# A retention and HGRN2 decoder layer: the last product of the down projection in two pieces of tokens, 256 and then 128

## The chip, the cores and the metric

The kernel runs on one core of a Trainium2 chip. The metric is the time of one execution on the device in microseconds; the kernel before has a median of 2376.54 us over three runs (2375.79 to 2379.05). Engines are named as in the profile: PE is TensorE's matmuls, PEld its weight loads, DVE VectorE, ACT ScalarE, POOL GpSimd, SP SyncE, which issues the DMAs here.

## What is computed

One layer of a decoder over 2048 tokens of a prompt and 8 samples of 8 tokens, width 1024. The part that matters here is the end of the layer: the squared-ReLU MLP with its residual, and the final norm.

```python
xp = xp + mp
hp = rmsnorm(xp, norm_ffn_w[l])
xp = xp + jnp.square(jax.nn.relu(hp @ w_up[l])) @ w_down[l]
...
y_prompt = rmsnorm(xp, final_norm_w)
```

The norm divides each token by the root of the mean of its 1024 squares and multiplies by one weight per column, so no token can leave before all 1024 of its columns are there.

## The kernel before, in words

Activations lie transposed: a column of the model on a partition, tokens along the free dimension. The 2112 tokens are cut into three groups (576, 768 and 768), which pass the MLP one after the other. A group is cut into two halves of T2 tokens (384 in the last group), and each large product is computed by a Strassen-like scheme of seven products on quarters of the operands. Operands are split into a rounded part `hi` and the rest `lo`, both fp32r, and a product is three matmuls: hi with hi, hi with lo, lo with hi.

`down` (L2185) is the down projection. For each of four steps `o` it runs seven such products, `LAST_OCTET` in the last step. The results are kept in slabs `g.R[v][q]`, each with two blocks of 128 columns of the model side by side; `last_block(g, n, h)` (L2360) is block `n` of half `h`. The very last of the 28 products is ("A12", "B21"). In the last group it is taken out of the loop and computed by `last_product` (L2242), and it concerns the four blocks 0 to 3 of half 0 alone, for 384 tokens each. Everything else has its final value by then: half 1 is finished by `finish` (L2276, multiplications at L2302, stores at L2304), and blocks 4 to 7 of half 0 have their squares summed in `g.sq` and their final weight multiplied in by `last_rows` (L2338).

`last_product` takes four PSUM banks, one per block (tiles called `pj` and `pf`), makes 12 matmuls of 384 columns into each (helper line L1849), and adds the result to the residual on DVE (L2259). Beside this, `finish_last` (L2364) works off the norm of half 0. It sets steps by `later(d, fn)`, at d ticks from its call; a tick is two matmuls. The steps are:

- `squares` (L2375): the squares of blocks 0 and 1 on ACT (L2377), plus `g.sq` on DVE (L2378).
- `weigh` (L2372): the final weight of a block on ACT (L2373).
- `split`: the two halves of that sum are added on DVE (L2018), rounded on ACT (L670), and the rest taken on DVE (L671).
- `square` of blocks 2 and 3, one by one, on ACT (L2385).
- `add` and `sums`: sums over the partitions by matmuls with ones on TensorE; the two squares in f32 (L2394), the two rounded parts in fp32r (L2389), all four into one bank `pj`.
- `outs` (L2396): the factor by a logarithm and an exponential on ACT (L2335, L2336), then for each pair of blocks one multiplication of 128 x 768 on DVE (L2401) and one store of 384 KB by SP (L2402).

The kernel is recorded by a scheduler: steps are put to the engines in the order in which it places them, each engine works off its own queue strictly in order, and a wait holds all that stands behind it on that engine.

Of the kernel before, what the change touches and what calls it, by code (L numbers as in the profile page):

```python
# [12 lines left out]
AF = mybir.ActivationFunctionType  # L13
ALU = mybir.AluOpType

P = 128
# [37 lines left out]
NO = NQ // 2  # L54

N_VAL = 4
N_MADE = 4
LEADS = (slice(0, 256), slice(256, WT))
N_KEPT = W_OUT0 + 4
# [146 lines left out]
class Kernel:  # L206
# [958 lines left out]
    def values_direct(self, g, p, b):  # L1165
# [7 lines left out]
        assert n <= len(banks)  # L1173
        for m in range(N_VAL):
            w = self.next_weight()
# [1065 lines left out]

    def last_product(self, g, B):  # L2242

        nc, T2 = self.nc, g.T // 2
        w = [self.next_weight(), self.next_weight()]

        banks = [self.mm(T2) for _ in range(4)]
        self.finish_last(g)
        for v in range(2):
            for i in range(2):  # L2250
                ps = banks[2 * v + i]
                for e in range(2):
                    for f in range(2):
                        c = (2 * e + f) * 256 + i * P
                        for q, (a, b) in enumerate(((0, 0), (0, 1), (1, 0))):
                            self.matmul(ps, w[v][a][:, c:c + P], self.pair(g, g.d[NO - 1][e][B][b])[:, f],
                                        start=e == f == q == 0, stop=e == f == 1 and q == 2)
                r = self.last_block(g, 2 * v + i, 0)
                nc.vector.tensor_tensor(out=r, in0=ps, in1=r, op=ALU.add)  # L2259

    def ffn(self, g, nxt, wait=0):
        g.u = {}
# [98 lines left out]
        np_, i = divmod(n, 2)  # L2361
        return self.pair(g, g.R[np_ % 2][np_ // 2, h])[:, i]

    def finish_last(self, g):  # L2364


        nc, w = self.nc, g.T // 2
        x = {}
        b2 = lambda t: t[:, :2 * w].rearrange("p (i t) -> p i t", i=2)
        block = lambda n: self.last_block(g, n, 0)  # L2370

        def weigh(n):  # L2372
            nc.scalar.activation(block(n), block(n), AF.Copy, scale=self.vec[:, V_FIN + n:V_FIN + n + 1])  # L2373

        def squares():  # L2375
            t = x["sum"] = self.get()
            nc.scalar.activation(b2(t), self.pair(g, g.R[0][0, 0]), AF.Square)  # L2377
            nc.vector.tensor_tensor(out=b2(t), in0=b2(t), in1=self.pair(g, g.sq), op=ALU.add)  # L2378

        def split():  # L2380
            x["parts"] = self.pair_parts(g, x["sum"])

        def square(n):
            x[n] = self.get()
            nc.scalar.activation(x[n][:, :w], block(n), AF.Square)  # L2385

        def sums():
            for part in x["parts"]:
                nc.tensor.matmul(x["ps"], self.ones_r, part, start=False, stop=False)  # L2389

        def add(n):
            if n == 2:
                x["ps"] = self.mm(w)
            nc.tensor.matmul(x["ps"], self.ones, x[n][:, :w], start=n == 2, stop=n == 3)  # L2394

        def outs():  # L2396
            t = self.get()
            self.last_factor(x["ps"], t[:, :w])
            for np_ in range(4):
                r = self.pair(g, g.R[np_ % 2][np_ // 2, 0])  # L2400
                nc.vector.tensor_tensor(out=r, in0=r, in1=t[:, :w].unsqueeze(1).to_broadcast([P, 2, w]), op=ALU.mult)  # L2401
                nc.sync.dma_start(self.outputs(g, 0)[:, 2 * np_:2 * np_ + 2], r)  # L2402

        for d, fn, *a in ((13, squares), (14, weigh, 0), (15, weigh, 1), (17, split), (19, square, 2), (23, add, 2),
                          (25, square, 3), (26, weigh, 2), (27, weigh, 3), (28, sums), (29, add, 3), (30, outs)):
            self.later(d, fn, *a)


# [61 lines left out]
```

## Time and profile before

| what | value |
|---|---|
| median of three runs (lowest, highest) | 2376.54 us (2375.79, 2379.05) |
| span of the profiled execution, first to last instruction | 2374.9 us |
| mean granted TensorE clock over the span | 0.998 |
| PE, PEld, DVE, ACT busy | 99%, 97%, 76%, 52% |
| from the last product's first matmul to the end of the span | 22.3 us |
| from its last result to the end of the span | 13.8 us |

The time of the profiled execution itself is not given apart from its span; the runs are other executions. Busy shares are means over the whole program. The change lies in the last one per cent of it, so the rows of that stretch are what is to be read: the windows and the timeline from 2352 us on, and the chain that ends last.

### The profile page before, as it was taken

The numbers are of one execution on the slowest core, as the hardware profiler recorded it, in microseconds if no ns is written. First come the engines' busy times: TensorE is split into PE (matmuls) and PEld (weight loads), VectorE is DVE, ScalarE is ACT, GpSimd is POOL, SyncE is SP. The second block draws the span as 40 slices with busy tenths as digits, with TensorE's granted clock in tenths as the row PEclk, the third lists the DMA queues.
The fourth block names the chain that finished last, engine by engine and source line by source line (L and its number), as shares of the span: only waits on it lengthen the run. The fifth ranks groups of instructions, "written<-read, shape, count | busy, mean of one in ns | idle before, by whom it ended". The sixth has DMA issues, their size and how long they took to land.

```text
span 2374.9 us, 39309 instructions
## 1 busy us (share of the span) xinstructions
PE 2348.4 (99%) x15322; PEld 2308.2 (97%) x15322; DVE 1795.9 (76%) x2299; ACT 1230.7 (52%) x1974; POOL 149.6 (6%) x202
## 2 busy tenths in 40 slices
PE   9999999999999999999999999999999999999998
PEld 8888799999999999999999999999999999999997
DVE  8666776777766766668769998666998786669887
ACT  5555565556655565536455556444544364445443
POOL 4222201101101010000000000000000000000000
PEclk9999999999999999999999999999999999999999
DMA  8888797778965787898777765766655458675641
GB/s 289 288 293 287 251 317 256 261 286 302 321 236 204 283 293 254 332 315 320 230 245 263 232 217 175 256 210 222 234 188 195 146 193 265 199 235 177 206 154 67
DMA packets 232505, 575.60 MB, mean 242 GB/s; under 512 B 24179, under 2 KB 92659, under 8 KB 232310
## 3 DMA queue, kind: packets, MB, share of 16 engines
q1 hardware_dynamic: 232166, 572.98, 70.7%
q8 instruction: 122, 2.00, 0.3%
q14 instruction: 73, 0.60, 0.1%
q10 hardware_dynamic: 144, 0.02, 0.0%
HBM read 419.95 MB, written 151.66 MB: 241 GB/s over the span
## 4 chain that ended last, share of the span: by engine, by line
PE 90%; DVE 3%; DMA 3%; ACT 2%; issue 1%; POOL 1%; SPq 0%; DVEq 0%; ACTq 0%
PE pj L1849 36%; PE pf L1849 28%; PE pj L452 9%; PE pj L1108 9%; PE pj L1192 2%; PE mm L1689 1%; PE mm L1697 1%; PE mm L1691 1%; PE mm L1466 1%; PE mm L1192 1%; PE mm L1619 1%; PE mm L1377 1%; PE mm L1838 1%; DMA raw<-w 0%; DMA ld<-fo 0%
## 5 line engine op out<-in xcount | busy, mean ns | idle before, releaser
L1849 PE MATMUL pj<-slab,hi 128*128 128x384 f32 (+1 forms) x3504 | 853.7, 326 | 1.1 <-ACT slab L1031 0.8
L310 ACT CAST hi<-raw 128x1024 fp32r<-128x1024 f32 (+1 forms) x449 | 471.0, 1049 | 681.4 <-PE pj L1849 266.7
L318 DVE TENSOR_TENSOR lo<-raw,hi 128x1024 fp32r<-128x1024 f32 (+1 forms) x449 | 549.6, 1224 | 164.1 <-ACT hi L310 152.6
L1849 PE MATMUL pf<-slab,hi 128*128 128x384 f32 (+1 forms) x2768 | 652.4, 321 | 0.0
L1849 PEld LDWEIGHTS pj<-slab,hi 128*128 128x128 f32 x3504 | 614.6, 188 | 1.7 <-ACT slab L1031 1.2
L1849 PE MATMUL pj<-slab,lo 128*128 128x384 f32 (+1 forms) x1752 | 570.5, 326 | 0.0
L1849 PEld LDWEIGHTS pf<-slab,hi 128*128 128x128 f32 x2768 | 480.6, 188 | 0.1
L1849 PE MATMUL pf<-slab,lo 128*128 128x384 f32 (+1 forms) x1384 | 443.1, 320 | 0.0
L1849 PEld LDWEIGHTS pj<-slab,lo 128*128 128x128 f32 x1752 | 329.3, 188 | 0.0
L1108 PE MATMUL pj<-hi,slab 128*128 128x256 f32 x1344 | 261.5, 287 | 2.0 <-DVE slab L1123 1.1
L1849 PEld LDWEIGHTS pf<-slab,lo 128*128 128x128 f32 x1384 | 260.1, 188 | 0.0
L452 PE MATMUL pj<-slab,hi 128*128 128x288 f32 (+1 forms) x1280 | 257.1, 316 | 1.7 <-ACT slab L716 0.9
L1108 PEld LDWEIGHTS pj<-hi,slab 128*128 128x128 f32 x1344 | 215.2, 191 | 3.1 <-ACT slab L1439 1.0
L452 PEld LDWEIGHTS pj<-slab,hi 128*128 128x128 f32 x1280 | 204.8, 189 | 5.4 <-issue 1.9
L1108 PE MATMUL pj<-lo,slab 128*128 128x256 f32 x672 | 190.1, 283 | 0.1
L1941 ACT CAST slab<-slab 128x768 fp32r<-128x768 f32 (+1 forms) x192 | 145.6, 780 | 63.9 <-DVE slab L1952 47.4
L1945 DVE TENSOR_TENSOR slab<-slab 128x768 fp32r<-128x768 f32 (+1 forms) x192 | 167.5, 887 | 13.2 <-ACT slab L1941 4.7
L452 PE MATMUL pj<-slab,lo 128*128 128x288 f32 (+1 forms) x640 | 149.4, 314 | 0.3 <-DVE lo L318 0.3
L1108 PEld LDWEIGHTS pj<-lo,slab 128*128 128x128 f32 x672 | 128.7, 191 | 0.3 <-DMA lo<-fki1VA12lo 0.3
L452 PEld LDWEIGHTS pj<-slab,lo 128*128 128x128 f32 x640 | 107.6, 188 | 0.7 <-DVE lo L318 0.6
L2195 DVE TENSOR_TENSOR slab<-pf,slab 128x768 f32<-128x768 f32 (+1 forms) x87 | 76.6, 885 | 24.4 <-PE pf L1849 24.3
L2195 DVE TENSOR_TENSOR slab<-pj,slab 128x768 f32<-128x768 f32 (+1 forms) x79 | 70.1, 889 | 20.5 <-PE pj L1849 20.3
(269 smaller groups left out, 2615.4 us busy)
## 6 DMA issues: line engine op xcount, KB each, us to landing
raw<-w SPq DMA_DIRECT2D x255, 512.0 KB, 4.7
slab<-fu SPq DMA_DIRECT2D x64, 384.0 KB, 5.2
fu<-ld SPq DMA_DIRECT2D x60, 384.0 KB, 4.1
ld<-x SPq DMA_DIRECT2D x40, 384.0 KB, 5.1
ld<-fin SPq DMA_DIRECT2D x28, 384.0 KB, 4.9
slab<-fu SPq DMA_DIRECT2D x32, 288.0 KB, 4.6
fu<-ld SPq DMA_DIRECT2D x30, 288.0 KB, 3.2
fres<-slab SPq DMA_DIRECT2D x16, 384.0 KB, 5.0
```

What stands on the lines that cost most here:

```text
L310: self.nc.scalar.copy(self.wts[j][0][:, c], raw[:, c])
L318: self.nc.vector.tensor_tensor(out=lo[:, c], in0=raw[:, c], in1=hi.bitcast(F32)[:, c], op=ALU.subtract)
L452: self.nc.tensor.matmul(pj[:, i, :T2], w, a[:, c0:c1], start=j == 0 and q == 0, stop=j == n - 1 and q == 2)
L1108: self.nc.tensor.matmul(ps[:, tb * 256:(tb + 1) * 256], t, w[:, cols], start=first and kb == j == 0 and tb != 1, stop=kb == KB // 2 - 1 an ...
L1192: nc.tensor.matmul(dst, t[:, s:s + C], ww, start=kb == 0 and q == 0, stop=last and q == 2, skip_group_check=True)
L1377: nc.tensor.transpose(ps[:, j * P:(j + 1) * P], src[:, c], self.ident)
L1466: nc.tensor.matmul(ps[:, j * P:(j + 1) * P], k[:, cols[c]], q[:, cols[c]], start=True, stop=True)
L1619: nc.tensor.matmul(ps[:, j * P:(j + 1) * P], rk[:, cols[c]], rq[:, cols[c]], start=True, stop=True)
L1849: self.nc.tensor.matmul(*a, **k)
L1941: self.nc.scalar.copy(hi[:, :g.T], B[name][:, :g.T])
L1945: self.nc.vector.tensor_tensor(out=lo[:, :g.T], in0=B[name][:, :g.T], in1=hi.bitcast(F32)[:, :g.T], op=ALU.subtract)
L2195: nc.vector.tensor_tensor(out=r, in0=ps, in1=r, op=ALU.add)
```

## The change

The 384 tokens of the last product are cut into `ENDS`, 256 and 128. For each piece in turn `last_product` calls `finish_last` for that piece and makes all 48 matmuls of the piece, so that 48 matmuls of 384 columns become 48 of 256 and 48 of 128. A block's two pieces go to the two banks of one double tile (`tile2`), and the piece's sum over the partitions goes to unused columns 256 and on of the first bank of tile `k` (tile 0 for the first piece, tile 1 for the second). The norm, the multiplications and the stores are made per piece: 8 multiplications and 8 stores, of 256 KB and 128 KB, instead of 4 and 4. `outs` becomes `factor` and four steps `out`, set two ticks apart.

```diff
@@ -54,6 +54,7 @@
 NO = NQ // 2
 
 N_VAL = 4
+ENDS = ((0, 256), (256, 384))
 N_MADE = 4
 LEADS = (slice(0, 256), slice(256, WT))
 N_KEPT = W_OUT0 + 4
@@ -2241,22 +2242,23 @@
 
     def last_product(self, g, B):
 
-        nc, T2 = self.nc, g.T // 2
+        nc = self.nc
         w = [self.next_weight(), self.next_weight()]
 
-        banks = [self.mm(T2) for _ in range(4)]
-        self.finish_last(g)
-        for v in range(2):
-            for i in range(2):
-                ps = banks[2 * v + i]
-                for e in range(2):
-                    for f in range(2):
-                        c = (2 * e + f) * 256 + i * P
-                        for q, (a, b) in enumerate(((0, 0), (0, 1), (1, 0))):
-                            self.matmul(ps, w[v][a][:, c:c + P], self.pair(g, g.d[NO - 1][e][B][b])[:, f],
-                                        start=e == f == q == 0, stop=e == f == 1 and q == 2)
-                r = self.last_block(g, 2 * v + i, 0)
-                nc.vector.tensor_tensor(out=r, in0=ps, in1=r, op=ALU.add)
+        tiles = [self.tile2() for _ in range(4)]
+        for k, (c0, c1) in enumerate(ENDS):
+            self.finish_last(g, c0, c1, tiles[k][:, 0, 256:256 + c1 - c0])
+            for v in range(2):
+                for i in range(2):
+                    ps = tiles[2 * v + i][:, k, :c1 - c0]
+                    for e in range(2):
+                        for f in range(2):
+                            c = (2 * e + f) * 256 + i * P
+                            for q, (a, b) in enumerate(((0, 0), (0, 1), (1, 0))):
+                                self.matmul(ps, w[v][a][:, c:c + P], self.pair(g, g.d[NO - 1][e][B][b])[:, f, c0:c1],
+                                            start=e == f == q == 0, stop=e == f == 1 and q == 2)
+                    r = self.last_block(g, 2 * v + i, 0)[:, c0:c1]
+                    nc.vector.tensor_tensor(out=r, in0=ps, in1=r, op=ALU.add)
 
     def ffn(self, g, nxt, wait=0):
         g.u = {}
@@ -2361,24 +2363,27 @@
         np_, i = divmod(n, 2)
         return self.pair(g, g.R[np_ % 2][np_ // 2, h])[:, i]
 
-    def finish_last(self, g):
-
-
-        nc, w = self.nc, g.T // 2
+    def finish_last(self, g, c0, c1, ps):
+
+
+        nc, w = self.nc, c1 - c0
         x = {}
         b2 = lambda t: t[:, :2 * w].rearrange("p (i t) -> p i t", i=2)
-        block = lambda n: self.last_block(g, n, 0)
+        two = lambda t: self.pair(g, t)[:, :, c0:c1]
+        block = lambda n: self.last_block(g, n, 0)[:, c0:c1]
 
         def weigh(n):
             nc.scalar.activation(block(n), block(n), AF.Copy, scale=self.vec[:, V_FIN + n:V_FIN + n + 1])
 
         def squares():
             t = x["sum"] = self.get()
-            nc.scalar.activation(b2(t), self.pair(g, g.R[0][0, 0]), AF.Square)
-            nc.vector.tensor_tensor(out=b2(t), in0=b2(t), in1=self.pair(g, g.sq), op=ALU.add)
+            nc.scalar.activation(b2(t), two(g.R[0][0, 0]), AF.Square)
+            nc.vector.tensor_tensor(out=b2(t), in0=b2(t), in1=two(g.sq), op=ALU.add)
 
         def split():
-            x["parts"] = self.pair_parts(g, x["sum"])
+            both = b2(x["sum"])
+            nc.vector.tensor_tensor(out=both[:, 0], in0=both[:, 0], in1=both[:, 1], op=ALU.add)
+            x["parts"] = self.parts(both[:, 0], w)
 
         def square(n):
             x[n] = self.get()
@@ -2386,23 +2391,23 @@
 
         def sums():
             for part in x["parts"]:
-                nc.tensor.matmul(x["ps"], self.ones_r, part, start=False, stop=False)
+                nc.tensor.matmul(ps, self.ones_r, part, start=False, stop=False)
 
         def add(n):
-            if n == 2:
-                x["ps"] = self.mm(w)
-            nc.tensor.matmul(x["ps"], self.ones, x[n][:, :w], start=n == 2, stop=n == 3)
-
-        def outs():
-            t = self.get()
-            self.last_factor(x["ps"], t[:, :w])
-            for np_ in range(4):
-                r = self.pair(g, g.R[np_ % 2][np_ // 2, 0])
-                nc.vector.tensor_tensor(out=r, in0=r, in1=t[:, :w].unsqueeze(1).to_broadcast([P, 2, w]), op=ALU.mult)
-                nc.sync.dma_start(self.outputs(g, 0)[:, 2 * np_:2 * np_ + 2], r)
-
-        for d, fn, *a in ((13, squares), (14, weigh, 0), (15, weigh, 1), (17, split), (19, square, 2), (23, add, 2),
-                          (25, square, 3), (26, weigh, 2), (27, weigh, 3), (28, sums), (29, add, 3), (30, outs)):
+            nc.tensor.matmul(ps, self.ones, x[n][:, :w], start=n == 2, stop=n == 3)
+
+        def factor():
+            x["t"] = self.get()
+            self.last_factor(ps, x["t"][:, :w])
+
+        def out(np_):
+            r = two(g.R[np_ % 2][np_ // 2, 0])
+            nc.vector.tensor_tensor(out=r, in0=r, in1=x["t"][:, :w].unsqueeze(1).to_broadcast([P, 2, w]), op=ALU.mult)
+            nc.sync.dma_start(self.outputs(g, 0)[:, 2 * np_:2 * np_ + 2, c0:c1], r)
+
+        for d, fn, *a in ((13, squares), (14, weigh, 0), (15, weigh, 1), (17, split), (19, square, 2), (23, add, 2), (25, square, 3),
+                          (26, weigh, 2), (27, weigh, 3), (28, sums), (30, add, 3), (31, factor),
+                          (34, out, 0), (36, out, 1), (38, out, 2), (40, out, 3)):
             self.later(d, fn, *a)
 
 
```

Where the steps stand in the queues is told by the built program. Slabs 21266 and 21381 hold blocks 0 and 1 and blocks 2 and 3, slabs 21320 and 21448 blocks 4 to 7; `pj_24550`, `pj_24551`, `pf_24552` and `pf_24553` are the product's four tiles, slab 24593 the first sum of squares, 24674 the second piece's, and 24640, 24654 and 24721 hold the factors. On DVE, the end of the queue from the add of block 2 on, before:

```order
L2259 TENSOR_TENSOR slab_21381<-pf_24552,slab_21381 128x384
L2018 TENSOR_TENSOR slab_24593<-slab_24593 128x384
L2259 TENSOR_TENSOR slab_21381<-pf_24553,slab_21381 128x384
L671 TENSOR_TENSOR slab_24607<-slab_24593,slab_24607 128x384
L2401 TENSOR_TENSOR slab_21266<-slab_21266,slab_24640 128x768
```

And the end of the same queue now, from the adds of the second piece's first two blocks on:

```order
L2261 TENSOR_TENSOR slab_21266<-pj_24551,slab_21266 128x128
L2405 TENSOR_TENSOR slab_21266<-slab_21266,slab_24654 128x2x256
L2405 TENSOR_TENSOR slab_21381<-slab_21381,slab_24654 128x2x256
L2381 TENSOR_TENSOR slab_24674<-slab_24674,slab_24518 128x256
L2405 TENSOR_TENSOR slab_21320<-slab_21320,slab_24654 128x2x256
L2405 TENSOR_TENSOR slab_21448<-slab_21448,slab_24654 128x2x256
L2385 TENSOR_TENSOR slab_24674<-slab_24674 128x128
L2261 TENSOR_TENSOR slab_21381<-pf_24552,slab_21381 128x128
L672 TENSOR_TENSOR slab_24692<-slab_24674,slab_24692 128x128
L2261 TENSOR_TENSOR slab_21381<-pf_24553,slab_21381 128x128
L2405 TENSOR_TENSOR slab_21266<-slab_21266,slab_24721 128x2x128
```

The second piece's halving add (L2385) and its adds of blocks 2 and 3 (L2261) stand behind the first piece's four multiplications (L2405). On PE, the end of the last product before, with the sums by ones behind it:

```order
L1849 MATMUL pf<-slab,hi 128x384 x2
L1849 MATMUL pf<-slab,lo 128x384
L2394 MATMUL pj<-slab,ones 128x384
L2389 MATMUL pj<-slab,ones_r 128x384 x2
L2394 MATMUL pj<-slab,ones 128x384
```

And now, from the eighth matmul of the second piece on; the fences show the first piece's sums, and then the end:

```order
L1850 MATMUL pj<-slab,hi 128x128 x2
L2397 MATMUL pj<-slab,ones 128x256
L1850 MATMUL pj<-slab,hi 128x128 x2
L1850 MATMUL pj<-slab,lo 128x128
```

```order
L1850 MATMUL pf<-slab,hi 128x128
L2397 MATMUL pj<-slab,ones 128x128
L1850 MATMUL pf<-slab,hi 128x128
L1850 MATMUL pf<-slab,lo 128x128
L2394 MATMUL pj<-slab,ones_r 128x128 x2
L2397 MATMUL pj<-slab,ones 128x128
```

The first piece's first sum by ones stands behind eight matmuls of the second piece, with the other 40 behind it; the second piece's first sum stands before the last two matmuls of the product.

## The prediction

> **What bounds the kernel now.** I read the page first, then the end of the program: busy time by stretch, the chain of waits, and the rows of the single operations. The page's span, busy times and chain by engine:
>
> ```profile
> span 2374.9 us, 39309 instructions
> PE 2348.4 (99%) x15322; PEld 2308.2 (97%) x15322; DVE 1795.9 (76%) x2299; ACT 1230.7 (52%) x1974; POOL 149.6 (6%) x202
> PE 90%; DVE 3%; DMA 3%; ACT 2%; issue 1%; POOL 1%; SPq 0%; DVEq 0%; ACTq 0%
> ```
>
> TensorE is the bound of the whole, but the change touches only the last product and what comes behind it. The stretches of that end (length, then busy time of PE, PEld, DVE, ACT and POOL, then granted clock, DMA share, GB/s) are cut at the product's first matmul, its last result, the first of the last multiplications, the issue of the last store, and its landing:
>
> ```profile
> 2352.55:2361.03 8.48, 8.48 (x49) 8.16 (x48) 7.34 (x13) 4.52 (x8) 0.00 (x0) 1.00 0.51 186
> 2361.03:2364.54 3.51, 1.98 (x7) 0.97 (x6) 1.02 (x2) 3.03 (x6) 0.00 (x0) 1.00 0.02 5
> 2364.54:2368.14 3.60, 0.00 (x0) 0.00 (x0) 3.56 (x4) 0.00 (x0) 0.00 (x0) 0.64 0.51 176
> 2368.14:2373.04 4.90, 0.00 (x0) 0.00 (x0) 0.00 (x0) 0.00 (x0) 0.00 (x0) 0.50 0.58 204
> 2373.04:2374.85 1.81, 0.00 (x0) 0.00 (x0) 0.00 (x0) 0.00 (x0) 0.00 (x0) 0.50 0.01 5
> ```
>
> Behind the last result lie 13.8 us: 3.5 of norm, 3.6 of multiplications, 4.9 until the last store has landed, 1.8 to the end. During the product itself DVE is busy for 7.34 of 8.48 us. That matters below. The chain through the norm, as start, length and operation:
>
> ```profile
> 2361.45 0.91 PE pj L2394 x2
> 2362.37 0.35 PE pj L2389 x2
> 2362.72 0.73 PE pj L2394 x2
> 2363.47 0.50 ACT slab L2335
> 2363.99 0.53 ACT slab L2336
> 2364.54 0.57 DVE slab L2401
> 2365.42 2.69 DVE slab L2401 x3
> ```
>
> The four sums, the logarithm and the exponential follow each other, then come four multiplications with a store each. The stores' rows (duration of the issue, then time to landing), for these four, for four equal ones that left over 6.1 us, and for 32 KB transfers:
>
> ```profile
> L2402 SPq DMA_DIRECT2D y<-slab x4: 372/372/1610, 2365.5 to 2368.1; - x4
> DMA to landing us min/median/max: 2.8/4.7/4.9
> ...
> L2304 SPq DMA_DIRECT2D y<-slab x4: 372/383/395, 2352.1 to 2358.2; - x4
> DMA to landing us min/median/max: 2.4/2.5/2.5
> ...
> L1320 SPq DMA_DIRECT2D ld<-slab x24: 507/588/596, 69.2 to 284.7; - x24
> DMA to landing us min/median/max: 1.9/3.5/5.3
> ```
>
> Alone a 384 KB store lands in 2.5 us; at one per 0.87 us they pile up to 4.9, and one issue is held for 1.61.
>
> **The change part by part.** First the matmuls. These are a run of 48 of 256 columns elsewhere (5.76 us), 48 of the product's own 384 columns (8.32 us), four f32 records of 128 columns, and all records of that line:
>
> ```profile
> 373.32:379.08 5.76, 5.76 (x49) 5.76 (x50) 1.00 0.81 278
> ...
> 2352.55:2360.87 8.32, 8.32 (x49) 8.16 (x48) 1.00 0.52 189
> ...
> 88.66 0.61 PE L1697 MATMUL mm<-slab 128*128 128x128 f32 x4
> ...
> L1697 PE MATMUL mm<-slab x256: 270/275/275, 88.7 to 1015.8; 128*128 128x128 f32 x128
> ```
>
> 48 wide ones take 5.76 us and end at 2358.31. For fp32r with 128 columns no row exists. From below: 0.173 to 0.120 is 0.053 less for 128 columns, so 0.067 each if that goes on, 3.2 us. From above: an f32 matmul of 128 columns is two records (256 for that line's 128 matmuls) of (0.61 - 0.275) / 3 = 0.112, so 0.22 each, 10.7 us. I take one such record, 0.11: it streams as many columns and loads as large a weight tile. That makes 5.3 us, 11.0 with the wide ones, 2.7 more than now on TensorE.
>
> The Trainium skill ("TensorE: Matmul & The Clock Gate", Back-to-back issue gap) gives about 81 ns for a sustained pair of weight load and matmul at 128 columns. By that figure the last store would leave 0.4 us earlier than in the sum below; no run here shows it.
>
> Now the vector and scalar operations, by the nearest sizes (duration in ns behind the bar's first number):
>
> ```profile
> L2401 DVE TENSOR_TENSOR slab<-slab 128x768 f32<-128x768 f32 x4 | 3.6, 953 | 2.4 <-ACT slab L2336 2.4
> L2302 DVE SCALAR_TENSOR_TENSOR slab<-slab,vec 128x384 f32<-128x384 f32 x8 | 4.7, 613 | 0.0
> ...
> L963 DVE TENSOR_TENSOR slab<-slab 128x512 f32<-128x512 f32 x4 | 2.7, 682 | 0.0
> L1620 DVE TENSOR_TENSOR slab<-mm,con 128x256 f32<-128x256 f32 x8 | 3.4, 424 | 5.3 <-PE mm L1619 5.1
> L1703 DVE TENSOR_TENSOR S<-slab,mm 128x128 f32<-128x128 f32 x60 | 16.9, 281 | 0.0
> ...
> L310 ACT CAST hi<-raw 128x256 fp32r<-128x256 f32 x1 | 0.4, 390 | 0.0
> L1721 ACT ACTIVATE dump<-mm 128x128 bf16<-128x128 f32 x128 | 35.0, 274 | 46.0 <-PE mm L1691 43.6 <-PE mm L1689 0.7
> ```
>
> In a full queue an operation costs about 0.085 less than its duration (four of 0.953 fill 3.56), so on DVE 0.87, 0.60, 0.34 and 0.20 for 768, 512, 256 and 128 columns, and 0.53 for L2302's kind. ACT takes 0.4 for 256 and 0.3 for 128 columns.
>
> *First piece.* The order on DVE, from the add at 2352.75 to the one that halves the squares (L2385 in the new text), is: two of 768, five of 0.53 (the other half's multiplications, still in the queue), one of 512 and four of 256: 1.74 + 2.65 + 0.60 + 1.36 = 6.35, no gap between, so it is done at 2359.2. Cast and square on ACT (0.32 + 0.40 with hand-overs of 0.03 to 0.05) release the first sum at 2360.0. TensorE by then has finished the wide matmuls and eight narrow ones (2359.2) and stands in front of that sum for 0.8. Then, in its order: the sum (0.45 and 0.1 for a load that nothing hides), eight narrow matmuls 0.88, two rounded sums 0.24, four narrow 0.44, the second sum 0.45: its result is there at 2362.7. The logarithm waits for DVE's narrow add of the same tile (0.28, L2261), which waits for that sum; then 0.40 and 0.40 make 2363.9. Now that point is 2364.5: the wide piece's factor comes only 0.6 earlier. Its four multiplications of 512, with the narrow piece's sum of squares (256) between, pass DVE by 2366.65; the stores leave from 2364.7 to 2366.8.
>
> *Second piece.* Its halving add and the adds that end its last two blocks stand on DVE behind all four of those multiplications: 2366.65 + 0.20 + 0.20. The square of block 2 is ready at 2367.5, and TensorE, which had reached that sum at 2365.4, has stood still for 2.1. Only then come the last two narrow matmuls (queued behind the sum), their add (2368.55), square (2368.9), sum (2369.4), logarithm and exponential (2370.1), and four multiplications of 0.34. SP needs about 0.46 per store (0.372 and a wait), so it is the slower of the two: stores at 2370.6, 2371.1, 2371.5 and 2372.0. Stepped in the same way, the order of now has its last store at 2368.1, as in the trace.
>
> *End.* The last store leaves 3.85 later (2372.0 against 2368.14). It carries 128 KB and finds little ahead of it: between the 1.9 of 32 KB and the 2.5 of a lone 384 KB I take 2.2 instead of 4.9. From landing to end 1.81 stays. In all -2.7 + 3.85 = +1.15. Adds, squares, weighings and casts of the second piece that are not named (some 16 more operations) run while another engine is waited for; uncovered, the eight on ACT would cost at most 8 x 0.3 = 2.4 us.
>
> The span becomes 2374.85 + 1.15 = 2376.0. The median of the runs, 2376.54 (2375.79 to 2379.05), lies 1.7 above the profiled span; I add the same 1.15 to it: 2377.7. About 0.2%, 4.75 us, is what a measurement of this kernel can tell from no change, so this is "the same".
>
> **The rivals.**
>
> 1. *Narrow matmuls at the f32 rate* (slower). If fp32r with 128 columns needs the two records of f32, 0.22, TensorE itself holds the narrow piece: the first piece's factor comes 1.4 later, the last matmul is done near 2371, the last store leaves at 2374.4: +6.3 - 2.7 = +3.6, 2380.1. For it: f32 does pay it at this size; no fp32r row is narrower than 256. Against: from 384 to 256 columns the price falls with the columns. It would pass 4.75 from about 0.25 per matmul on, or if the last store also took 4.9 to land (+6.3).
>
> 2. *The waits do not bind* (faster). If the second piece followed its own matmuls: 2358.3 + 5.3 + 1.1 for the first piece's sums = 2364.7, a norm of 2.5 instead of 3.5, stores to 2369.0, then 2.2 and 1.8: 2373.0, -1.8, 2374.7. For it: this is what TensorE alone would allow. Against: on DVE the second piece's adds are queued behind the first piece's multiplications.
>
> 3. *The last landing does not shorten* (the stores do not do what the smaller size promises): 4.9 again, +3.85, 2380.4. For it: the 1.61 issue was held by something in the transfer engines, and 32 KB took 5.3 at worst. Against: 2.4 to 2.5 in all four spaced stores, which are three times as large.
>
> One more price belongs to my own case, the clock after TensorE's stand of 2.1 us. This stretch of now begins 2.06 after the last sum's result (2363.44; PEclk 0.56):
>
> ```profile
> 2365.50:2366.00 0.50, 0.00 (x0) 0.00 (x0) 0.50 (x2) 0.00 (x0) 0.00 (x0) 0.56 0.04 16
> ```
>
> So the clock can halve at just that length of idleness; the last sums and the two narrow matmuls, 0.6 in all, would then take 0.6 more (+1.75, 2378.3). The Trainium skill (the same page, What's actually happening) names a free-running idle window of about 3.4 us, by which a stand of 2.1 would often pass unpunished; the trace's 2.1 is the shorter and says that it need not.
>
> **How the numbers follow.** My case has 0.55 (with the halved clock inside it), rival 1 0.2, rival 2 0.1, rival 3 0.15. All four stay within 4.75 us of now; beyond it lie rivals 1 and 3 together (+6.3), or a narrow matmul dearer than f32's, for which I keep 0.06, and on the other side no mechanism that I can price, 0.02. That leaves 0.92 for no change. The range reaches up to rival 3 (2380.4) and down past the scatter of the runs under my case to half of rival 2's way (2375.5).
>
> **What the profile would show.** Right: L2406's first four stores near 2364.7 to 2366.8 and its last near 2372; landings of the last about 2.2 after their issue; PEld idle twice in front of L2397, about 0.8 and 2.1, each ended by ACT's L2390; DVE's narrow adds of the last two blocks behind its four multiplications of 512; the 48 narrow matmuls at about 0.11 each. Wrong: narrow matmuls at 0.22 and no second stand of TensorE (rival 1); the second piece's adds done before 2366 (rival 2); a last landing of over 4 (rival 3). A span more than 4.75 from 2374.9 would say that the end hangs on something that none of these rows shows.

## The result, and the profile after

The changed kernel is slower: a median of 2383.49 us over ten runs (2381.55 to 2385.97) against 2377.03 for ten runs of the kernel before (2375.1 to 2379.05). The ratio is 1.0023, 95% interval 1.0015 to 1.0031, so +0.23%. Ten more runs of the changed kernel gave 2381.85, against 32 of the kernel before a ratio of 1.0021 (1.0012 to 1.0031). The prediction said 2377.7 with a range up to 2380.4; the time lies above it.

From here on "before" and "after" are the two kernels, and numbers without a unit are microseconds. The span of the profiled execution of after is 2382.2. It is 7.3 longer than before's 2374.85, but the last product also begins 2.54 later, at 2355.09 instead of 2352.55, after instructions that stand in the same order. So I count from the product's first matmul to the end of the span and call that the tail: 22.30 before, 27.07 after. The change costs 4.8 there in this pair of executions.

The busy times by stretch, with the columns as in the prediction. The cuts are the product's start, the end of the wide matmuls, the result of the first piece's last sum, the second piece's first sum, its last sum, the issue of the last store, and the end of its transfers, but for a small rest:

```profile
2355.09:2360.84 5.75, 5.75 (x50) 5.75 (x50) 5.63 (x12) 3.34 (x6) 0.00 (x0) 1.00 0.52 190
2360.84:2365.26 4.42, 3.73 (x31) 3.48 (x29) 1.65 (x5) 2.00 (x6) 0.00 (x0) 1.00 0.32 113
2365.26:2370.11 4.85, 2.85 (x27) 2.70 (x26) 4.06 (x10) 2.34 (x8) 0.00 (x0) 0.91 0.42 139
2370.11:2372.75 2.64, 2.33 (x8) 1.85 (x8) 0.34 (x2) 1.09 (x3) 0.00 (x0) 0.50 0.42 143
2372.75:2375.74 2.99, 0.00 (x0) 0.00 (x0) 1.43 (x4) 0.59 (x2) 0.00 (x0) 0.50 0.22 58
2375.74:2378.35 2.61, 0.00 (x0) 0.00 (x0) 0.00 (x0) 0.00 (x0) 0.00 (x0) 0.50 0.59 162
2378.35:2382.16 3.81, 0.00 (x0) 0.00 (x0) 0.00 (x0) 0.00 (x0) 0.00 (x0) 0.50 0.01 2
```

Two rows are not as forecast: the fourth, at half the clock, and the last, 3.81 without any work to speak of before the end. The chain of waits through the second norm (start, length, operation) shows the queues that were forecast:

```profile
2366.47 1.29 DVE slab L2405 x2
2367.77 0.34 DVE slab L2381
2368.10 1.21 DVE slab L2405 x2
2369.31 0.21 DVE slab L2385
...
2370.11 0.79 PE pj L2397 x2
...
2371.94 0.81 PE pj L2397 x2
```

The second piece's halving add (L2385) stands behind all four multiplications of 512, and TensorE stands until 2370.11. Now the end of SP's queue: the stores, the reading of the flag that says whether the second pass is needed (TENSOR_LOAD, L613), the branch over that pass, and what came next. These rows are after's, by source line:

```profile
L2406 SPq DMA_DIRECT2D y<-slab x8: 372/372/786, 2367.2 to 2375.7; - x8
...
DMA to landing us min/median/max: 2.0/2.2/2.6
...
L613 SPq TENSOR_LOAD <-flag x1: 486/486/486, 2376.2 to 2376.2; - x1
...
L2456 SPq EVENT_SEMAPHORE  x8: 17/17/17, 2380.2 to 2380.8; - x8
...
L2456 SPq COMPARE_BRANCH  x1: 50/50/50, 2376.8 to 2376.8; - x1
```

SP's next instruction behind its branch runs only at 2380.25. The waits of SP's queue name that stand, here of after and then of before (waited for, total, times, longest):

```profile
SPq L2456 <- SPq L2456: 3.4, 1, 3.4
```

```profile
SPq L2451 <- SPq L2451: 2.5, 1, 2.5
```

So before's trace had it too, with its branch at 2370.35 and SP's next instruction at 2372.93:

```profile
L2451 SPq EVENT_SEMAPHORE  x8: 17/17/17, 2372.9 to 2373.5; - x8
...
L2451 SPq COMPARE_BRANCH  x1: 50/50/50, 2370.4 to 2370.4; - x1
```

And the last store's landing? The rows of the stores give a landing for three of the four in before and for six of the eight in after, and the last is not among them. But the trace holds the sixteen steps of the semaphore that the last store raises, and the other landings are taken from such steps as well. In before the sixteenth step comes at 2373.01, 4.87 after the issue and 0.1 after SP's next instruction; the prediction had seen only the landing. In after fifteen steps have come by 2377.64, 1.9 after the issue, but the sixteenth comes at 2379.38, 3.64 after it. From 2377.24 to 2378.39 one instruction transfer of 16 KB and three of 8 KB run. So the small store landed later than its 2.2, and SP stood for 0.87 longer still.

The issue of the sixth store took 0.786, while a 16 KB instruction transfer (queue q8) ran; this is the use of the DMA queues from 2373.8 to 2374.8:

```profile
q8 instruction: 1, 0.02, 5.5%
```

5.5% of 16 engines over 1.0 us is one engine for 0.88. All kernels of this study follow, from one trace each. All but the start and the median are counted from the product's start: the first store of the second norm piece (where the product is in pieces too), the last issue, its landing by the semaphore's sixteenth step, and SP's next instruction behind the branch:

| kernel | product's start | second piece's first store | last issue | its landing | SP's next | tail | median of runs |
|---|---|---|---|---|---|---|---|
| before | 2352.55 | | 15.59 | 20.46 | 20.38 | 22.30 | 2377.03 |
| before, again | 2354.78 | | 15.58 | 20.47 | 20.06 | 22.31 | 2377.46 |
| after | 2355.09 | 18.79 | 20.65 | 24.29 | 25.16 | 27.07 | 2383.49 |
| after, again | 2351.35 | 18.65 | 20.26 | 24.23 | 24.20 | 26.12 | 2381.85 |
| before, no branch | 2353.27 | | 15.58 | 18.67 | | 19.74 | 2374.71 |
| after, no branch | 2356.52 | 18.78 | 20.29 | 22.19 | | 23.15 | 2377.38 |
| multiplications later | 2352.57 | 17.94 | 19.51 | 23.76 | 23.80 | 25.71 | 2380.86 |
| 20 matmuls, waiting tile | 2351.67 | 20.85 | 22.75 | 26.20 | 26.83 | 28.75 | 2385.14 |
| 20 matmuls, free tile | 2357.56 | 18.04 | 20.28 | 23.85 | 24.17 | 26.09 | 2381.36 |
| both mendings | 2352.13 | 17.64 | 20.05 | 24.00 | 23.90 | 25.82 | 2380.03 |
| matmuls alone in pieces | 2355.57 | | 20.00 | 24.70 | 24.40 | 26.54 | 2383.09 |
| norm and stores alone | 2353.18 | | 17.09 | 20.02 | 20.89 | 22.81 | 2377.79 |
| last store by ACT | 2352.79 | | 15.59 | 20.33 | 20.05 | 22.17 | 2376.76 |

In eight of the eleven traces with the branch the end comes 1.9 after SP's next instruction; a landing up to 0.1 later than that makes no difference there. In the other three, all with four whole stores of 384 KB, the landing is 0.3 to 0.4 later than SP's next instruction, and the end comes 1.84 after the landing. The product starts anywhere from 2351.35 to 2357.56 (mean 2353.8), in repeats of one kernel too.

### The profile page after: what moved, and what is told of

The parts are those of the page before. It is cut to its first block, busy times and chain, and to the rows that moved or that the text cites. A ratio compares the mean times of both kernels' runs of the same rounds, so it can differ in the third digit from the quotient of the medians.

```text
span 2382.2 us, 39445 instructions
## 1 busy us (share of the span) xinstructions
PE 2353.6 (99%) x15376; PEld 2314.5 (97%) x15376; DVE 1796.4 (75%) x2310; ACT 1231.7 (52%) x1984; POOL 147.4 (6%) x202
## 4 chain that ended last, share of the span: by engine, by line
PE 86%; DVE 1%; DMA 1%; ACT 1%; POOL 0%; issue 0%; SPq 0%; DVEq 0%; ACTq 0%
PE pj L1850 36%; PE pf L1850 28%; PE pj L1109 9%; PE pj L453 7%; PE mm L1690 1%; PE mm L1692 1%; PE mm L1698 1%; PE mm L1839 1%; PE mm L1467 0%; PE mm L1620 0%; PE mm L1378 0%; DMA ld<-fo 0%; PE pj L1193 0%; DMA ld<-x 0%; DVE slab L1422 0%
## 5 line engine op out<-in xcount | busy, mean ns | idle before, releaser
L1850 PE MATMUL pf<-slab,hi 128*128 128x384 f32 (+2 forms) x2784 | 654.3, 320 | 0.0
L1850 PE MATMUL pf<-slab,lo 128*128 128x384 f32 (+2 forms) x1392 | 445.1, 320 | 0.0
L2196 DVE TENSOR_TENSOR slab<-pf,slab 128x768 f32<-128x768 f32 (+1 forms) x87 | 76.5, 884 | 24.4 <-PE pf L1850 24.2
```

The lines of the kernel that those rows point to most:

```text
L1850: self.nc.tensor.matmul(*a, **k)
```

## The experiments

**1 and 2. Both kernels without the branch.** The theory (A): the end hangs on SP's branch, not on the landing alone. The edit takes out three things together, in both kernels: the reading of the flag, the branch, and the second pass that it skips.

```diff
-            if self.fast:
-                self.again = nc.values_load(self.flag, min_val=0, max_val=1,
...
-        with tc.If(fast.again > 0):
-            Kernel(tc, I, O, False).build()
```

> The kernel before without the test of the flag and without the second pass that the test skips; the pass that runs is the same (it leaves out the repair for inputs that need it, which these do not). The tail is counted from the first matmul of the last product to the end of the span: 22.3 us before, 27.1 after. Theory A (the end hangs on SP: after its last store issue it reads the flag in 0.49, branches, and needs 2.5 to 3.4 until its next instruction, and 1.9 more to the end): the fourth issue of L2402 takes 0.37 instead of 1.61, no 16 KB instruction transfer runs beside the stores, the last store lands about 3.8 after its issue, and the tail is about 21.3 (15.6 + 3.8 + 1.9). Theory B (the end hangs on the last landing alone, as the prediction had it, and the branch costs nothing): landing 4.9 after the issue again, tail 22.3.

> The kernel after without the test of the flag and without the second pass that it skips. Theory A: the stretch from SP's last issue to its next wait, 4.1 us after (flag 0.49, branch, 3.4 of standing), goes; the issue of the sixth store takes 0.37 instead of 0.79; the end follows the last landing by 1.9. Last issue 20.2 after the product's start, landing 2.0 to 2.3, tail 24.2 to 24.4 instead of 27.1, so about 2.8 less. Theory B (the branch costs nothing, the 3.8 us between the last landing and the end belong to the number of stores that have to be waited for): tail 26.6 to 27.1. Time against the kernel before, whose branch stays: A +1.9 in the tail, B +4.5.

The stores before without the branch, with the landings of three of the four, and SP's wait at the end, which now is for a store:

```profile
L2399 SPq DMA_DIRECT2D y<-slab x4: 372/372/373, 2366.2 to 2368.8; - x4
...
DMA to landing us min/median/max: 2.5/2.7/2.9
```

```profile
SPq L2445 <- DMA y<-slab: 2.7, 1, 2.7
```

The same after without the branch, with the landings of six of the eight:

```profile
L2403 SPq DMA_DIRECT2D y<-slab x8: 372/373/443, 2368.6 to 2376.8; - x8
...
DMA to landing us min/median/max: 1.9/2.2/2.3
```

```profile
SPq L2450 <- DMA y<-slab: 1.3, 3, 0.5
```

The tails are 19.74 and 23.15: A, and by more than it said (21.3 and 24.2 to 24.4). Without the branch the long issues are gone (1.61 and 0.79 became 0.37 and 0.41). The last store, by its semaphore, lands 3.09 after its issue in before and 1.90 in after, where it was 4.87 and 3.64, and the end follows that landing by 1.0 to 1.1. So the branch costs twice: it holds SP, and with it the stores land later. The times: 2374.71, ratio 0.9987 (0.9977 to 0.9996) against before, and 2377.38, ratio 1.0002 (0.9993 to 1.0012). In the tail the branch costs 2.6 in before and 3.0 to 3.9 in after, by after's two traces. Between the two kernels lie 3.8 to 4.8 with it and 3.4 without it; the medians say 4.4 to 6.5 and 2.7. Here the smaller last store shortens the stretch from the last issue to the end by 1.3 (4.16 to 2.86); with the branch it is 0.3 to 0.9 (6.71 to 6.42 or 5.86).

By the tail, the larger part of the loss is thus not the branch's. Experiments 3 to 8 are about that part.

**3. The first piece's multiplications later.** They are set 16 ticks later, so that fewer of them stand in front of the second piece's adds:

```diff
-            self.later(d, fn, *a)
+            self.later(d + (16 if fn is out and c0 == 0 else 0), fn, *a)
```

> The kernel after with the first piece's four multiplications set 16 ticks later. On DVE the second piece's halving add then stands behind two of them instead of four, and its two late adds each behind one more. Theory A (the prediction's entanglement: each wide multiplication ahead of those adds costs its 0.60): the second piece's first sum starts about 1.2 earlier, TensorE stands 1.0 instead of 2.2 in front of it, its clock stays whole, and the second factor is there 1.85 earlier (0.75 of it the clock's); tail 27.1 - 1.9 = 25.2 if the branch is as long as after's. Theory B (TensorE's narrow matmuls or the scalar engine hold the second piece, not DVE): the second factor comes within 0.3 of where it is after, tail 26.8 to 27.4.

The second piece's first store came at 17.94, 0.7 to 0.85 earlier than in the two traces of after, not 1.85. The tail is 25.71, the time 2380.86, ratio 1.0016 (1.0007 to 1.0026). The stretch from TensorE's stand on (PEclk is the third column from the right):

```profile
2365.60:2367.10 1.50, 0.00 (x0) 0.00 (x0) 1.50 (x5) 0.58 (x2) 0.00 (x0) 1.00 0.87 294
2367.10:2367.70 0.60, 0.52 (x5) 0.52 (x5) 0.29 (x1) 0.43 (x2) 0.00 (x0) 1.00 1.00 331
2367.70:2368.30 0.60, 0.57 (x4) 0.38 (x3) 0.29 (x1) 0.09 (x1) 0.00 (x0) 0.51 0.69 236
```

The stand went from 2.0 to 1.6, so the entanglement is real, but it is smaller than said, and the clock fell all the same, after TensorE had gone back to work. A's direction held and its size did not; B is out.

**4 and 5. The stand filled with work.** Matmuls of ones in front of the second piece's first sum, first into a tile that a late add still had to read, then into one that was free:

```diff
         def add(n):
+            if c0 and n == 2:
+                for _ in range(20):
+                    nc.tensor.matmul(warm, self.ones_r, self.ones_r, start=True, stop=True)
```

> The kernel after with 20 more matmuls of ones (128 columns, fp32r, into unused columns of a bank that nothing reads) in front of the second piece's first sum, 2.24 us at 0.112, about as long as TensorE stands there. Theory A (the stand halves the clock, and that costs 0.75 in the last sums and the two matmuls between them): the granted clock stays 1.0, the stretch from the second piece's first sum to its last result takes 1.9 instead of 2.65, tail 26.35. Theory B (those rows are slow for another reason, as waits for the two late adds): the stretch stays near 2.6, tail 27.1.

> As the run with 20 matmuls of ones, but into columns of the first tile, which was read for the last time long before TensorE gets there; in that run they went into a tile that still waited for a late add, so they stood behind the wait and filled nothing. Now they run directly behind the 46th narrow matmul, 2.24 us at 0.112 over a stand of 2.1 to 2.2. Theory A (the stand halves the clock, and that costs 0.75): granted clock 1.0 up to the last sum, the stretch from the second piece's first sum to the last sum's result 1.9 instead of 2.65, last PE record 16.5 after the product's start instead of 17.2, tail 26.3. Theory B (the clock falls at times of its own, whatever is busy, as it fell in that run after 2 us of full work): clock 0.5 in the last sums again, last PE record near 17.2, tail 27.1.

The first of the two missed: its matmuls waited for that add, filled nothing and made the tail 1.7 longer (five runs, 2385.14, ratio 1.0035, 1.0021 to 1.0049). It showed something else: TensorE stood from 2364.8 to 2366.3, worked at full clock for 2.1, and only then was halved:

```profile
2364.80:2366.30 1.50, 0.00 (x0) 0.00 (x0) 1.50 (x4) 0.17 (x1) 0.00 (x0) 1.00 1.02 337
2366.30:2368.40 2.10, 2.05 (x18) 2.05 (x19) 0.29 (x1) 0.74 (x3) 0.00 (x0) 1.00 0.72 243
2368.40:2371.00 2.60, 2.30 (x12) 2.12 (x11) 0.29 (x1) 0.71 (x2) 0.00 (x0) 0.51 0.00 0
```

The second did what it should: the 20 matmuls fill the stand, and then comes the stretch of the second piece's sums:

```profile
2370.35:2372.60 2.25, 2.25 (x22) 2.25 (x22) 2.09 (x6) 0.56 (x3) 0.00 (x0) 1.00 0.92 300
2372.60:2374.50 1.90, 1.36 (x10) 1.03 (x9) 0.33 (x2) 1.07 (x4) 0.00 (x0) 1.00 0.58 196
```

This stretch takes 1.9 at clock 1.00, against 2.64 at 0.50 in after (2.5 in its second trace). That is A: 0.6 to 0.75 for the clock, and the last sum's second record started 16.6 after the product's start (16.5 expected). Of the seven traces with the product and the norm in pieces, the five in which TensorE stands there for 1.6 or more lost the clock before the last sum was done; this one and experiment 8, where the stand is filled, kept it. That speaks for A, though the moment of the fall also follows a clock of its own (last section). The 0.6 to 0.75 reached the second piece's first store (18.04). The next issue then took 1.11 beside a 16 KB transfer, so the tail (26.09) lies 1.0 below the one trace of after and level with the other; the time is 2381.36, ratio 1.0017 (1.0008 to 1.0026).

**6. Matmuls and adds alone in pieces**, norm, multiplications and stores whole:

```diff
-        for v in range(2):
+        for k, (c0, c1) in enumerate(((0, 256), (256, 384))):
+            if k:
+                self.finish_last(g)
+            for v in range(2):
```

> One part of the change alone: the matmuls and the adds of the last product in pieces of 256 and 128, norm, multiplications and stores whole as before. Theory A (TensorE's price alone): 48 x (0.120 + 0.112 - 0.173) = 2.8 more until the last result, the rest as before, tail 22.3 + 2.8 = 25.1 with the branch at SP's end as in the kernel before; the other 2.0 of the change's 4.8 then belong to norm and stores by pieces. Theory B (four more adds on DVE and the order of its queue hold the norm beyond that): tail 26 or more, and nearly all of the change's loss lies in the matmuls and adds.

The tail is 26.54, the time 2383.09, ratio 1.0025 (1.0015 to 1.0034): B. The chain of waits shows the cause, from the last narrow matmuls of block 1 to the first sum, and TensorE's waits beside it:

```profile
2361.48 2.65 PE pj L1849 x24
...
2364.15 0.30 DVE slab L2261
...
2364.48 0.85 ACT slab L2379
...
2365.36 0.97 DVE slab L2380
...
2366.35 0.57 DVE slab L2018
...
2366.94 0.51 ACT slab L670
2367.45 0.43 ACT slab L2387
...
2367.93 0.91 PE pj L2396 x2
```

```profile
PE pj L2396 <- ACT slab L2387: 1.9, 2, 1.4
```

The first two blocks' second piece is added at 2364.15, and squares, add, halving, cast and square take 3.8 from there to the first sum. In before, 24 matmuls of 0.173, 4.2, follow the add's tile; here 24 of 0.112, 2.7. So TensorE reaches the sum early and stands 1.4 in front of it. The clock stays whole here (1.00 up to the last sum). The last issue is 4.4 later than before: 2.8 for the rate of narrow matmuls, as expected, and the other 1.6 goes with this stand and with the sum that stands ahead of the last two matmuls. That is almost the whole delay of the change's last issue (20.00 against 20.26 and 20.65).

**7. Norm, multiplications and stores alone in pieces**, matmuls whole:

```diff
-            self.finish_last(g, c0, c1, tiles[k][:, 0, 256:256 + c1 - c0])
+            self.finish_last(g, c0, c1, tiles[k][:, 1, :c1 - c0])
+        for c0, c1 in ((0, 384),):
...
-                    ps = tiles[2 * v + i][:, k, :c1 - c0]
+                    ps = tiles[2 * v + i][:, 0, :c1 - c0]
```

> The other part of the change alone: the 48 matmuls and four adds whole, 384 columns, as before; norm, multiplications and stores in pieces of 256 and 128, so that the last store carries 128 KB. Multiplications 4 x 0.60 + 4 x 0.34 instead of 3.56 and eight issues of 0.46: last issue about 16.0 after the product's start instead of 15.6. Theory A (the end hangs on SP's branch behind its last issue, 5.8 to 6.7 from that issue to the end in six kernels so far, whatever the stores carry): tail 21.8 to 22.7. Theory B (the prediction's term: the small last store lands in 2.2 instead of 4.9 and the end follows it by 1.8): 16.0 + 2.2 + 1.8 = 20.0.

Both norms are set at the same ticks here, so that the multiplications of the two pieces alternate instead of following each other: the run tries the small last store, not the second norm behind the first. SP's stores, and its branch with what came next:

```profile
L2407 SPq DMA_DIRECT2D y<-slab x8: 372/452/1629, 2365.1 to 2370.3; - x8
```

```profile
L2457 SPq EVENT_SEMAPHORE  x8: 17/17/17, 2374.1 to 2374.6; - x8
...
L2457 SPq COMPARE_BRANCH  x1: 50/50/50, 2371.5 to 2371.5; - x1
```

The tail is 22.81, the time 2377.79, ratio 1.0000 (0.9990 to 1.0009). B's 20.0 is out: a last store of 128 KB behind an unchanged product does not bring the end nearer. It lands 2.93 after its issue, not 2.2, and SP's stand behind its branch is 2.5 again (2371.5 to 2374.1) and ends 0.87 after that landing. The tail is 0.1 above A's range, because the seventh issue took 1.63 (beside a 16 KB transfer again), which puts the last one at 17.1 instead of 16.0.

**8. Both mendings of the change**, 3 and 5 together with 15 matmuls:

> Both mendings of the change together: the first piece's multiplications 16 ticks later, and 15 matmuls of ones (1.7 us) in front of the second piece's first sum. Theory A (the two losses add up): last PE record at about 15.9 after the product's start (16.4 with the first alone, 16.6 with the second alone, 17.1 to 17.2 with neither), last issue 19.0, tail 24.8 to 25.7, so still 2.5 or more longer than before, because TensorE's 2.8 and the second norm behind the first remain. Theory B (one of them hides the other): tail 25.7 to 26.1, as with the better one alone.

The tail is 25.82, just above A's range and in B's; one issue took 1.33, which is 0.9 more than its neighbours took. The second piece's first store is the earliest of all (17.64, against 17.94 and 18.04), so the two do not hide each other, but they do not add up in full either (1.15 from after's 18.79, where the single ones gave 0.85 and 0.75). The time is 2380.03, ratio 1.0012 (1.0003 to 1.0021): still slower than before.

**9. Before, with the last store issued by the scalar engine:**

```diff
-                nc.sync.dma_start(self.outputs(g, 0)[:, 2 * np_:2 * np_ + 2], r)
+                (nc.scalar if np_ == 3 else nc.sync).dma_start(self.outputs(g, 0)[:, 2 * np_:2 * np_ + 2], r)
```

> The kernel before with its last store issued by the scalar engine instead of SP, so that SP reads the flag and branches behind the third store, 0.9 to 2.1 us earlier, while the scalar engine branches behind the fourth. Theory A (the end hangs on the branch of whichever engine issues last): SP's next instruction 18.6 after the product's start; the scalar engine's issue at 15.6, 0.4 to 1.6 long, flag 0.47, 2.9 of standing, so 19.4 to 20.6; SP's waits for the stores pass beside it, and 0.9 to 1.3 are left: tail 20.3 to 21.9, middle 21.2, about 1.1 less than now. Theory B (the last landing sets the end): tail 22.3 within 0.3.

The scalar engine's store with the landings of the three that SP issued, and the branches of the two engines with what came next:

```profile
L2402 ACTq DMA_DIRECT2D y<-slab x1: 414/414/414, 2368.4 to 2368.4; - x1
...
DMA to landing us min/median/max: 2.8/4.6/4.7
```

```profile
L2451 SPq EVENT_SEMAPHORE  x8: 17/17/17, 2372.8 to 2373.6; - x8
...
L2451 SPq COMPARE_BRANCH  x1: 50/50/50, 2368.8 to 2368.8; - x1
L2451 ACTq COMPARE_BRANCH  x1: 54/54/54, 2369.7 to 2369.7; - x1
L2451 ACTq EVENT_SEMAPHORE  x1: 17/17/17, 2372.8 to 2372.8; - x1
```

The tail is 22.17, the time 2376.76, ratio 0.9997 (0.9987 to 1.0006): no gain. SP branched 1.6 earlier and stood 4.0 instead of 2.5, until the scalar engine's stand ended too; and the last store, by its semaphore, landed at 2373.1 again, 4.74 after its issue. A's price was wrong. B's number came out, although experiment 1 shows that the branch is not free: the stands ended at 2372.8 and the landing 0.3 later, too close together to tell the two theories apart by the tail.

**10 and 11. The two kernels once more.**

> The kernel after once more, unchanged, to tell the tail from the scatter ahead of it. Its order ahead of the last product is that of before, so the product's start should scatter as in the other runs (2351.7 to 2356.5 so far) and the tail be 27.1 within 0.5 (theory A: the change costs 4.8, and what the medians show beyond it, 1.7, is scatter; the median of these runs then comes near 2382.2). Theory B (the change also costs some 1.7 ahead of the last product): start again near 2355, median again near 2383.5.

> The kernel before once more, unchanged: how far its tail scatters. Theory A (of the 22.3 the stretch from the last issue to the end, 6.7, is branch and landing side by side, and scatters by some tenths, as it does in the kernels with pieces, 5.8 to 6.5): tail 21.4 to 22.5, product's start anywhere from 2351 to 2357. Theory B (the start of the product is the same in each run of this kernel, and later in the changed one): start within 0.5 of 2352.55.

After, run again, has its product's start at 2351.35, a tail of 26.12 and a time of 2381.85. Before, run again, has its start at 2354.78, a tail of 22.31, a last stretch of 6.73, which scatters less than was said, and a time of 2377.46, ratio 0.9999 (0.9990 to 1.0008). So the start scatters by several us in both (A's part on the start holds in both), but after's tail lies 0.5 below the 26.6 to 27.6 that A gave it, so the tail scatters by about 1. The cost of the change in the tail is 3.8 to 4.8. That lies inside the interval of both ratios (0.15% to 0.31% of 2377 are 3.6 to 7.4); that the first median lies 6.5 higher needs no other cause, and none was shown. In before again no issue was held (four of 0.37), and its last store still landed 4.89 after its issue: the late landing does not hang on the held issue.

## Why the prediction was wrong

Its steps, counted from the product's start, with the end of the wide matmuls first:

| step | predicted | after |
|---|---|---|
| wide matmuls done | 5.76 | 5.75 |
| first piece's first sum starts | 7.45 | 7.44 |
| first piece's last sum there | 10.15 | 10.17 |
| first store, fourth store | 12.15, 14.25 | 12.10, 14.25 |
| second piece's first sum starts | 14.95 | 15.02 |
| its last sum there | 16.85 | 17.66 |
| last store issued | 19.45 | 20.65 |
| last store landed | 21.65 | 24.29 |
| end | 23.45 | 27.07 |

**What was right.** The queues, up to the second sum, to 0.1. The narrow matmul, for which there was no row, was taken at 0.11; in the kernel with the free tile 22 of them take 2.46 and 20 more 2.23 in the chain of waits, 0.112 each:

```profile
2368.11 2.46 PE pf L1850 x22
2370.57 2.23 PE pj L2399 x20
```

Rival 1 (0.22) is out, and so is the Trainium skill's 81 ns ("TensorE: Matmul & The Clock Gate", Back-to-back issue gap): this trace has 112. Rival 2 is out: the second piece's adds did queue behind the first piece's multiplications, and TensorE stood twice.

**The step that failed** is the end: "From landing to end 1.81 stays. In all -2.7 + 3.85 = +1.15." The stretch from the last issue to the end was to shrink by 2.7 and shrank by 0.3 (6.71 to 6.42; by 0.85 in the second trace). Two terms of it were wrong, and both hang on SP's branch.

The first is the landing, taken as 2.2 instead of 4.9. It came 3.64 after the issue (3.97 in the second trace) instead of 4.87. The 4.9 in its row was another store's, and that the last one took as long was luck. The prediction put the 4.9 down to stores that pile up at one per 0.87. In experiment 1 the same four stores leave at the same pace without the branch, and the last lands in 3.09: piling up explains 0.6 over a lone store's 2.5, and 1.8 came with the branch. The small store pays that as well (3.64 against 1.90 without the branch). So rival 3, a landing that does not shorten, was half right, and of the single cases its +3.85 came nearest.

The second is the wait beside the landing, which the sum did not have. Behind its last issue SP reads the flag (0.48 to 0.88 in these runs) and branches over the second pass; its next instruction comes 2.5 to 4.0 later, and the end 1.9 after that. In before the landing and that stand ended 0.1 apart, so that the trace looked as if the landing alone set the end; its waits of SP, which say "SPq L2451 <- SPq L2451: 2.5", were not read. Experiments 1, 2 and 7 show it: take the branch away, and the small store is worth 1.3; keep it and make only the store small, and the tail does not shrink.

The Trainium skill has the rule that was missed ("Runtime: NRT & Kernel Launch", Instruction fetch mechanics): a taken branch to code that is not yet loaded has to wait until it has been fetched. These stands, 2.5 to 4.0 on SP, agree with it, and so do the instruction transfers of 8 and 16 KB beside the last stores, of which the kernels without the branch have none. No run has a branch over a short body, so that the stand is the loading of code is argued here, not shown.

**What was priced but left in a corner.** The halved clock was in the text at 0.6 and cost 0.6 to 0.75 (experiment 5). The held issue was seen in before as 1.61 and not carried over: it comes with the branch, in some executions, and is gone without it. By the table the tail was 3.6 longer than forecast (27.07 - 23.45): 0.8 up to the last sum, most of it the clock, 0.4 more up to the last issue, 1.4 in the landing and 1.0 behind it. The range took such costs as cases of which one comes true at a time, and they came together; the last three all go with the branch. The median lies 5.8 above the forecast. The remaining 2.2 is 0.5 by which ten runs put before's own median higher than the three runs that the forecast started from, and 1.7 that is within the scatter of the product's start.

**What was right for too narrow a reason.** The +3.85 of the last issue was put down to narrow matmuls, 2.7, and to the two norms getting in each other's way. Experiment 6 gives 4.4 with one norm, from matmuls and adds in pieces alone: 24 narrow matmuls are too short a cover for the norm's chain of 3.8. Splitting norm and stores on top of that moved the last issue no nearer (20.26 and 20.65 against 20.00). Other cuts of the 384 tokens, the narrow piece first or two of 192, were not tried.

## What to carry to other kernels

The end of a program is a set of queues that finish side by side: before shortening the one that ends last, look for every other wait that ends within a few tenths of it, the issuing engine's own queue and its branch among them. Cutting a matmul's moving side from 384 to 256 and 128 columns costs 0.120 + 0.112 against 0.173 here, and the cover that the wide matmuls gave to the other engines' chain goes with it. Costs that have one cause belong in one case, added up, not in several cases of which only one may come true.

## What the runs showed of the hardware

- Behind this branch over code that is not run, every engine stands: SP 2.5 to 4.0 in eleven executions, GpSimd 2.6 in the middle of the program (before: branch at 1894.4, next instruction at 1897.1), and TensorE's branch is recorded as 3.4 to 4.0 long.
- A store's issue beside an instruction transfer of 8 or 16 KB can take 0.5 to 1.6 instead of 0.37; in after one of 0.37 ran beside a transfer of 16 KB as well. Without the branch there was no such transfer beside the stores and no issue over 0.44.
- With the branch the last store landed 2.9 to 4.3 (128 KB) or 4.7 to 4.9 (384 KB) after its issue, without it 1.9 and 3.1.
- The granted clock does not follow TensorE's idleness at a fixed distance. It fell 2.1 after the last matmul in before and 1.1 after it in after, whose rows are these:

```profile
2368.70:2369.20 0.50, 0.00 (x0) 0.00 (x0) 0.50 (x2) 0.00 (x0) 0.00 (x0) 1.00 1.05 356
2369.20:2369.70 0.50, 0.00 (x0) 0.00 (x0) 0.50 (x3) 0.16 (x1) 0.00 (x0) 0.53 1.00 322
```

  In experiment 4 it fell after 2.1 of full work. What the falls share is a grid: in each of the thirteen traces the clock's last fall lies a whole number of steps of 3.413 (691 to 695 of them) behind the first record of the clock, and that first record lies at another time in most executions (4.2 to 7.2 from the start). The Trainium skill's free-running window of about 3.4 ("TensorE: Matmul & The Clock Gate", Part 1: The HAM clock gate) agrees with that. The whole idle window that the same section asks for does not: a stand of 1.6 was enough (experiment 3).
- A rounded matmul of 128 columns takes 0.112, one of 256 columns 0.120: half the columns save 7%.
